# ReLU and row sum on one core: the first block cut from 16 to 15 rows a partition, so that all row pitches change

## The chip, the cores and the metric

The kernel runs on one core of one Trainium2 chip. The metric is the device time of one execution in microseconds (us), taken as the median over runs. Before the change it is 160.99 us, the median of three runs from 160.93 to 161.05.

## The reference

The input x has 32 x 512 x 1024 float32 numbers, 67.1 MB. The output has one float32 for each of the 16,384 rows of 1,024 numbers: the sum of the row after negative numbers were set to zero.

```
relu_x = np.maximum(x, 0)
return np.sum(relu_x, axis=-1)
```

Each number is read once and used twice (a maximum, an addition), so the work is a stream from the chip's memory (HBM) through the on-chip memory (SBUF) with very little written back.

## The kernel before, in words

The 16,384 rows are spread over 128 partitions, 128 rows (4 KB each) to a partition. The tensor is not cut evenly into 128 runs of 128 rows. It is cut in two regions (`xf` and `xv` in `relu_sum`). The first region holds 2,048 rows, and partition p gets 16 of them that follow each other in memory. So the rows of neighbouring partitions begin 64 KB apart: this distance is called the pitch. The second region holds the other 112 rows of each partition, again consecutive, at a pitch of 448 KB.

The work goes in blocks. Each of the seven blocks (`NB`) is one DMA load of 16 rows a partition, 64 KB to each partition and 8.4 MB in all, into one of three buffers `io0` to `io2`, which are used in turn. Block 0 is the first region; blocks 1 to 6 are the first 96 rows of the second region. The last 16 rows a partition are the **tail**, which is cut ever finer so that little is left to do after the last byte: a load of 8 rows, one of 4 rows, and four loads that share the last four rows: 2,302 numbers a partition (two rows and a piece of 254), 873 numbers (the far end of the four rows), 518 numbers, and 403 numbers, the last into a small buffer `last`.

All loads are issued by SyncE (SP) from one queue, in the order of the code (`load`, the DMA at L104). The first is moved ahead of the start of the program (`open_without_barrier`). Loads 0 to 2 wait for nothing; from the fourth on, a load waits until VectorE (DVE) is done with the block that was in the buffer (`freed`, a count of the semaphore `dve`). The first load of the tail waits so for block 4; those behind it wait only because SP issues in order.

The lists `TWO`, `ACT` and `DVE` say who computes each block. `TWO` lists groups of rows that pass through two engines: ScalarE (ACT) clamps the group in place (`clamp`, L145) and DVE adds it up (`total`, L153). `ACT` and `DVE` count rows that one engine does alone, clamp and sum in one instruction (`act_row`, L160; `dve_row`, L168). Blocks 0 and 1 are one group of 16, blocks 2 to 4 two groups of 8, block 5 two groups of 7 and two rows for ACT alone, block 6 eight rows for each engine alone. In the tail rows alternate between ACT and DVE; in the load of 8 rows the eighth goes to ACT too, so ACT has five and DVE three.

The last rows are computed in pieces: `act_part` (L122) and `dve_part` (L127) take the loads of 873 and 518 numbers, GpSimd (POOL) clamps a piece of 254 (L246), and one last DVE instruction (L266) and one last ACT instruction take the load of 403. Then SP stores the last two columns of `res` (`store`, L116). Two larger stores go before it. Eight matrix products (`multiply`, L186), whose result nobody reads, run on TensorE (PE) after the last block of the loop.

Of the kernel before, what the change touches and what calls it, by code (L numbers as in the profile page):

```python
# [4 lines left out]
F32 = mybir.dt.float32  # L5
RELU = mybir.ActivationFunctionType.Relu
MAX, ADD = mybir.AluOpType.max, mybir.AluOpType.add
P = 128

ROWS = 16  # L10
NBUF = 3


TWO = [[16], [16], [8, 8], [8, 8], [8, 8], [7, 7], []]
ACT = [0, 0, 0, 0, 0, 2, 8]
DVE = [0, 0, 0, 0, 0, 0, 8]

TAIL = [8, 4]  # L20

HEAD, MIDDLE = 254, 518
LAST_DVE, LAST_ACT = 252, 151
MIDDLE_ACT, END_ACT = 214, 321
# [29 lines left out]
class Semaphores:  # L56
    def __init__(self, tc: tile.TileContext):
        n = len(TWO) + len(TAIL) + 4
        self.loads = [tc.alloc_semaphore(f"load{i}") for i in range(n)]
        self.act = tc.alloc_semaphore("act")  # L60
        self.dve = tc.alloc_semaphore("dve")
        self.end = self.loads[-1]
        self.stored = tc.alloc_semaphore("stored")


def relu_sum(nc, sems: Semaphores, x: bass.AP, out: bass.AP):
    x_flat = x.flatten_outer_dims()
    N, D = x_flat.shape
    NT = N // P
    NB = len(TWO)  # L70
    assert N == P * NT == P * ROWS * (NB + 1)
    assert sum(TAIL) == ROWS - 4
    assert HEAD + MIDDLE + LAST_DVE == D and HEAD == 2 + LAST_DVE

    bufs = [nc.alloc_sbuf_tensor(f"io{i}", [P, ROWS, D], F32) for i in range(NBUF)]
    res = nc.alloc_sbuf_tensor("res", [P, NT], F32)


    n_last = LAST_DVE + LAST_ACT
    last = nc.alloc_sbuf_tensor("last", [P, 2 + n_last + 2], F32)  # L80


    N1 = P * ROWS
    xf = x_flat[:N1].rearrange("(p m) d -> p m d", p=P)
    xv = x_flat[N1:].rearrange("(p m) d -> p m d", p=P)
    o_flat = out.rearrange("b s -> (b s)")
    of = o_flat[:N1].rearrange("(p m) -> p m", p=P)
    ov = o_flat[N1:].rearrange("(p m) -> p m", p=P)

    def rows(m, n):  # L90
        if m < ROWS:
            return xf[:, m : m + n, :]
        return xv[:, m - ROWS : m - ROWS + n, :]

    def sums(m, n):
        if m < ROWS:
            return of[:, m : m + n], res[:, m : m + n]
        return ov[:, m - ROWS : m - ROWS + n], res[:, m : m + n]

    n_load = n_act = n_dve = n_store = 0  # L100

    def load(dst, src, after=None):
        nonlocal n_load
        dma = nc.sync.dma_start(out=dst, in_=src)  # L104
        if after:
            dma.wait_op(sems.dve, after[1], "sem-ge")
        dma.then_inc(sems.loads[n_load], 16)
        n_load += 1
        return sems.loads[n_load - 1]

    def store(m, n, act, sem, count):
        nonlocal n_store
        dst, src = sums(m, n)
        if act:
            nc.sync.wait_ge(sems.act, act)
        nc.sync.dma_start(out=dst, in_=src).wait_op(sem, count, "sem-ge").then_inc(  # L116
            sems.stored, 16
        )
        n_store += 1

    def act_part(ap, accum_out, after):
        nc.scalar.activation(out=ap, in_=ap, func=RELU, accum_out=accum_out).wait_op(  # L122
            *after, "sem-ge"
        ).then_inc(sems.end, 1)

    def dve_part(ap, accum_out, after):
        i = nc.vector.tensor_scalar(  # L127
            out=ap,
            in0=ap,
            scalar1=0.0,  # L130
            scalar2=None,
            op0=MAX,
            op1=ADD,
            accum_out=accum_out,
        )
        if after is not None:
            i.wait_op(*after, "sem-ge")
        i.then_inc(sems.end, 1)

    def clamp(ap, loaded):  # L140
        nonlocal n_act
        if n_act == 0:
            nc.scalar.preload_act_table(RELU).wait_op(loaded, 16, "sem-ge")  # L143
            loaded = None
        i = nc.scalar.activation(out=ap, in_=ap, func=RELU)  # L145
        if loaded is not None:
            i.wait_op(loaded, 16, "sem-ge")
        i.then_inc(sems.act, 1)
        n_act += 1

    def total(ap, m, n):
        nonlocal n_dve
        nc.vector.tensor_reduce(  # L153
            out=res[:, m : m + n], in_=ap, axis=mybir.AxisListType.X, op=ADD
        ).wait_op(sems.act, n_act, "sem-ge").then_inc(sems.dve, 1)
        n_dve += 1

    def act_row(ap, accum_out, loaded):
        nonlocal n_act
        i = nc.scalar.activation(out=ap, in_=ap, func=RELU, accum_out=accum_out)  # L160
        if loaded is not None:
            i.wait_op(loaded, 16, "sem-ge")
        i.then_inc(sems.act, 1)
        n_act += 1

    def dve_row(ap, accum_out, loaded):
        nonlocal n_dve
        i = nc.vector.tensor_scalar(  # L168
            out=ap,
            in0=ap,  # L170
            scalar1=0.0,
            scalar2=None,
            op0=MAX,
            op1=ADD,
            accum_out=accum_out,
        )
        if loaded is not None:
            i.wait_op(loaded, 16, "sem-ge")
        i.then_inc(sems.dve, 1)
        n_dve += 1  # L180

    def multiply(done):
        ps = nc.alloc_psum_tensor("ps", [P, MM_COLS], F32)
        rows_of = bufs[(NB - 2) % NBUF]
        for k in range(N_MM):
            i = nc.tensor.matmul(  # L186
                ps[:, :], rows_of[:, 0, :P], rows_of[:, 1, :MM_COLS], start=True, stop=True
            )
            if k == 0:
                i.wait_op(sems.dve, done, "sem-ge").then_inc(sems.end, 1)  # L190

    freed = []
    m = 0
    for j in range(NB):
        buf = bufs[j % NBUF]
        loaded = load(buf[:, :, :], rows(m, ROWS), j >= NBUF and freed[j - NBUF])
        c = 0
        act_waits = dve_waits = loaded
        for n in TWO[j]:
            clamp(buf[:, c : c + n, :], act_waits)  # L200
            total(buf[:, c : c + n, :], m + c, n)
            act_waits = None
            c += n
        for _ in range(ACT[j]):
            act_row(buf[:, c, :], res[:, m + c : m + c + 1], act_waits)
            act_waits = None
            c += 1
        for _ in range(DVE[j]):
            dve_row(buf[:, c, :], res[:, m + c : m + c + 1], dve_waits)
            dve_waits = None  # L210
            c += 1
        assert c == ROWS
        freed.append((n_act, n_dve))
        m += ROWS


    multiply(freed[-1][1])
    buf = bufs[NB % NBUF]
    c = 0
    for n in TAIL:  # L220
        loaded = load(
            buf[:, c : c + n, :], rows(m, n), None if c else freed[NB - NBUF]
        )
        for i in range(n):
            if i % 2 == 0 or (n == 8 and i == 7):
                act_row(buf[:, c, :], res[:, m : m + 1], loaded if i == 0 else None)
            else:
                dve_row(buf[:, c, :], res[:, m : m + 1], loaded if i == 1 else None)
            c += 1
            m += 1  # L230

    flat = buf[:, :, :].rearrange("p c d -> p (c d)")
    src = rows(m, 4).rearrange("p c d -> p (c d)")
    at = c * D
    head = 2 * D + HEAD
    middle = head + MIDDLE
    end = middle + n_last


    loaded = load(flat[:, at : at + head], src[:, :head])  # L240
    act_row(buf[:, c, :], res[:, m : m + 1], loaded)
    sums_act = n_act
    dve_row(buf[:, c + 1, :], res[:, m + 1 : m + 2], loaded)
    sums_dve = n_dve
# [1 line left out]
    nc.gpsimd.tensor_scalar(  # L246
        out=clamped, in0=clamped, scalar1=0.0, scalar2=None, op0=MAX
    ).wait_op(loaded, 16, "sem-ge").then_inc(sems.end, 1)
    for lo, hi, n, first, second in (
        (end, 4 * D, END_ACT, 2 + n_last, 3 + n_last),  # L250
        (head, middle, MIDDLE_ACT, 0, 1),
    ):
        loaded = load(flat[:, at + lo : at + hi], src[:, lo:hi])
        act_part(flat[:, at + lo : at + lo + n], last[:, first : first + 1], (loaded, 16))
        dve_part(flat[:, at + lo + n : at + hi], last[:, second : second + 1], (loaded, 16))
    loaded = load(last[:, 2 : 2 + n_last], src[:, middle:end])
    assert loaded is sems.end

    store(0, ROWS, freed[0][0], sems.dve, freed[0][1])
    store(ROWS, NT - ROWS - 2, sums_act, sems.dve, sums_dve)


    all_there = (sems.end, 16 + 6)
# [61 lines left out]
```

## Time and profile before

| what | before |
|---|---|
| time, median of three runs | 160.99 us (160.93 to 161.05) |
| span of the profiled execution, first to last instruction | 159.9 us |
| what lies around the span, if that execution took the median | 1.1 us |
| moved from HBM | 67.11 MB, 420 GB/s over the span |
| DMA packets' time as a share of 16 DMA engines | 97.8% |
| DVE busy | 118.7 us (74%) |
| ACT busy | 103.6 us (65%) |
| PE, POOL busy | 8.6 us, 1.0 us |

The time of the profiled execution itself is not recorded beside its span; sums are made against the span and carried over to the median with the 1.1 us unchanged. A packet here is one partition's share of one load, moved by one of the 16 DMA engines; a block of 16 rows is 128 packets of 64 KB, eight to each DMA engine. The chain of waits follows the work back from the last instruction, each step to what released it. The DMA view can be asked for a window of time: it divides the window into 40 slices, and its row "GB/s" puts the bytes of a packet into the slice in which the packet begins, so that in a short window the row shows when packets begin.

### The profile page before, as it was taken

How to read it: one execution, taken by the hardware profiler on the slowest of the kernel's cores; microseconds unless marked ns; L12 is line 12 of the kernel's file. 1: busy time of each engine (PE TensorE's matmuls, PEld its weight loads, DVE VectorE, ACT ScalarE, POOL GpSimd, SP SyncE). 2: the span in 40 equal slices, each digit the busy share in tenths (PEclk: the TensorE clock that was granted, in tenths of full speed). 3: DMA queues.
4: the chain of work that ended last, by engine and by line, in shares of the span. 5: the costliest groups of instructions: out<-in, count | busy, mean ns of one | idle time of the engine just before them, and what ended most of it. 6: DMA issues, size and time to landing. Idle time of an engine off the chain costs nothing.

```text
span 159.9 us, 157 instructions
## 1 busy us (share of the span) xinstructions
PE 8.6 (5%) x16; PEld 3.6 (2%) x16; DVE 118.7 (74%) x44; ACT 103.6 (65%) x53; POOL 1.0 (1%) x5
## 2 busy tenths in 40 slices
PE   0000000000000000000000000000000000000695
PEld 0000000000000000000000000000000000000241
DVE  0000000006999799999999999999999799999986
ACT  0000049993599807997099950999429993397995
POOL 0000000000000000000000000000000000000001
DMA  8996996996996997999979979969969969899993
GB/s 279 508 492 295 524 492 295 524 492 295 525 492 295 524 475 311 524 393 393 525 328 459 508 344 459 508 295 508 492 295 524 492 295 524 377 402 402 428 396 110
DMA packets 2304, 67.18 MB, mean 420 GB/s; under 512 B 640, under 2 KB 768, under 8 KB 1024
## 3 DMA queue, kind: packets, MB, share of 16 engines
q1 hardware_dynamic: 2304, 67.18, 97.8%
HBM read 67.11 MB, written 0.07 MB: 420 GB/s over the span
## 4 chain that ended last, share of the span: by engine, by line
DMA 45%; DVE 45%; ACT 9%; SPq 1%; issue 0%
DMA io<-in_x_dram 45%; DVE res L153 43%; ACT io L145 9%; DVE io L168 1%; SPq L104 1%; DVE io L127 1%; DVE io L266 0%
## 5 line engine op out<-in xcount | busy, mean ns | idle before, releaser
L153 DVE TENSOR_REDUCE res<-io 128x8 f32<-128x8192 f32 (+2 forms) x10 | 101.1, 10173 | 39.2 <-ACT io L145 39.2
L145 ACT ACTIVATE io<-io 128x8192 f32<-128x8192 f32 (+2 forms) x10 | 81.8, 8218 | 25.9 <-DMA io<-in_x_dram 25.9
L160 ACT ACTIVATE io<-io 128x1024 f32<-128x1024 f32 x18 | 18.8, 1042 | 6.6 <-DMA io<-in_x_dram 6.6
L186 PE MATMUL ps<-io 128*128 128x512 f32 x16 | 8.6, 698 | 149.5 <-DVE io L168 149.5
L168 DVE TENSOR_SCALAR_CACHE_REDUCE io<-io 128x1024 f32<-128x1024 f32 x14 | 16.2, 1215 | 0.5 <-DMA io<-in_x_dram 0.4
L143 ACT ACT_TABLE_LOAD x1 | 1.3, 1283 | 22.3 <-DMA io<-in_x_dram 22.3
L186 PEld LDWEIGHTS ps<-io 128*128 128x128 f32 x16 | 3.6, 231 | 153.7 <-DVE io L168 149.5
L160 ACT ACTIVATION_READ_ACCUMULATOR io<-io 128x1 f32 x18 | 3.3, 186 | 0.0
L246 POOL TENSOR_SCALAR io<-io 128x254 f32<-128x254 f32 x1 | 0.8, 841 | 155.4 <-DMA io<-in_x_dram 155.4
L168 DVE DVE_READ_ACCUMULATOR io<-io 128x1 f32 x14 | 1.2, 82 | 0.0
L127 DVE TENSOR_SCALAR_CACHE_REDUCE io<-io 128x552 f32<-128x552 f32 (+1 forms) x2 | 1.1, 594 | 0.0
L122 ACT ACTIVATE io<-io 128x321 f32<-128x321 f32 (+1 forms) x2 | 0.9, 426 | 0.1
L266 DVE SCALAR_TENSOR_TENSOR io<-last,io 128x254 f32<-128x254 f32 x1 | 0.4, 423 | 0.0
L122 ACT ACTIVATION_READ_ACCUMULATOR io<-io 128x1 f32 x2 | 0.4, 186 | 0.0
L122 ACT ACTIVATE last<-last 128x153 f32<-128x153 f32 x1 | 0.3, 330 | 0.0
L122 ACT ACTIVATION_READ_ACCUMULATOR last<-last 128x1 f32 x1 | 0.2, 187 | 0.0
L127 DVE DVE_READ_ACCUMULATOR io<-io 128x1 f32 x2 | 0.2, 82 | 0.0
L311 POOL MEMSET const-uint8-127<- 128x1 uint8 x1 | 0.1, 102 | 0.0
L311 POOL MEMSET const-bfloat16-1.0<- 128x1 bf16 x1 | 0.1, 101 | 0.0
L311 POOL MEMSET const-float32-0.0<- 128x1 f32 x1 | 0.1, 99 | 0.2 <-issue 0.2
L311 POOL MEMSET const-float32-1.0<- 128x1 f32 x1 | 0.1, 98 | 0.0
L266 DVE DVE_READ_ACCUMULATOR io<-last,io 128x1 f32 x1 | 0.1, 82 | 0.0
## 6 DMA issues: line engine op xcount, KB each, us to landing
io<-in_x_dram SPq DMA_DIRECT2D x1, 4096.0 KB, 23.7
io<-in_x_dram SPq DMA_DIRECT2D x1, 2048.0 KB, 28.3
io<-in_x_dram SPq DMA_DIRECT2D x1, 1151.0 KB, 30.6
io<-in_x_dram SPq DMA_DIRECT2D x1, 436.5 KB, 31.2
io<-in_x_dram SPq DMA_DIRECT2D x1, 259.0 KB, 31.4
last<-in_x_dram SPq DMA_DIRECT2D x1, 201.5 KB, 31.4
io<-in_x_dram SPq DMA_DIRECT2D x7, 29.0
out_dram<-res SPq DMA_DIRECT2D x1, 55.0 KB, 1.6
```

What stands on the lines that cost most here:

```text
L104: dma = nc.sync.dma_start(out=dst, in_=src)
L122: nc.scalar.activation(out=ap, in_=ap, func=RELU, accum_out=accum_out).wait_op(*after, "sem-ge").then_inc(sems.end, 1)
L127: i = nc.vector.tensor_scalar(out=ap, in0=ap, scalar1=0.0, scalar2=None, op0=MAX, op1=ADD, accum_out=accum_out,)
L143: nc.scalar.preload_act_table(RELU).wait_op(loaded, 16, "sem-ge")
L145: i = nc.scalar.activation(out=ap, in_=ap, func=RELU)
L153: nc.vector.tensor_reduce(out=res[:, m : m + n], in_=ap, axis=mybir.AxisListType.X, op=ADD).wait_op(sems.act, n_act, "sem-ge").then_inc(se ...
L160: i = nc.scalar.activation(out=ap, in_=ap, func=RELU, accum_out=accum_out)
L168: i = nc.vector.tensor_scalar(out=ap, in0=ap, scalar1=0.0, scalar2=None, op0=MAX, op1=ADD, accum_out=accum_out,)
L186: i = nc.tensor.matmul(ps[:, :], rows_of[:, 0, :P], rows_of[:, 1, :MM_COLS], start=True, stop=True)
L246: nc.gpsimd.tensor_scalar(out=clamped, in0=clamped, scalar1=0.0, scalar2=None, op0=MAX).wait_op(loaded, 16, "sem-ge").then_inc(sems.end, 1)
L266: nc.vector.scalar_tensor_tensor(out=clamped, in0=last[:, : 2 + LAST_DVE], scalar=0.0, in1=clamped, op0=MAX, op1=ADD, accum_out=res[:, NT ...
L311: nc = _bacc.Bacc("TRN2", target_bir_lowering=False, num_devices=1)
```

## The change

The first region gets 15 rows a partition in place of 16, so its pitch is 60 KB. The second region gets 113 rows at a pitch of 452 KB. Block 0 is 15 rows; blocks 1 to 6 stay at 16 rows; the tail grows from 16 rows to 17, and its first load from 8 rows to 9. Of these 9 rows ACT computes five and DVE four. As 17 rows do not fit in a buffer of 16, the load of 873 numbers goes to a buffer of its own, `ends`, and the two instructions on it work there. The stores are cut at 15 rows in place of 16. The rest of the last four rows is as before. Issue order, waits and semaphores stay.

```diff
+FIRST = 15
-TWO = [[16], [16], [8, 8], [8, 8], [8, 8], [7, 7], []]
+TWO = [[15], [16], [8, 8], [8, 8], [8, 8], [7, 7], []]
-TAIL = [8, 4]
+TAIL = [9, 4]
...
+    n_end = 2 * D - HEAD - MIDDLE - n_last
+    ends = nc.alloc_sbuf_tensor("ends", [P, n_end], F32)
-    N1 = P * ROWS
+    N1 = P * FIRST
     xf = x_flat[:N1].rearrange("(p m) d -> p m d", p=P)
     xv = x_flat[N1:].rearrange("(p m) d -> p m d", p=P)
...
-        loaded = load(buf[:, :, :], rows(m, ROWS), j >= NBUF and freed[j - NBUF])
+        n_rows = sum(TWO[j]) + ACT[j] + DVE[j]
+        loaded = load(buf[:, :n_rows, :], rows(m, n_rows), j >= NBUF and freed[j - NBUF])
...
-            if i % 2 == 0 or (n == 8 and i == 7):
+            if i % 2 == 0:
...
-    for lo, hi, n, first, second in (
-        (end, 4 * D, END_ACT, 2 + n_last, 3 + n_last),
-        (head, middle, MIDDLE_ACT, 0, 1),
+    for dst, lo, hi, n, first, second in (
+        (ends[:, :], end, 4 * D, END_ACT, 2 + n_last, 3 + n_last),
+        (flat[:, at + head : at + middle], head, middle, MIDDLE_ACT, 0, 1),
     ):
-        loaded = load(flat[:, at + lo : at + hi], src[:, lo:hi])
+        loaded = load(dst, src[:, lo:hi])
...
-    store(0, ROWS, freed[0][0], sems.dve, freed[0][1])
-    store(ROWS, NT - ROWS - 2, sums_act, sems.dve, sums_dve)
+    store(0, FIRST, freed[0][0], sems.dve, freed[0][1])
+    store(FIRST, NT - FIRST - 2, sums_act, sems.dve, sums_dve)
```

More of the change, by code (lines that the diff above doesn't have):

```diff
@@ L70, in relu_sum @@
     NB = len(TWO)
-    assert N == P * NT == P * ROWS * (NB + 1)
-    assert sum(TAIL) == ROWS - 4
+    assert N == P * NT
+    assert FIRST + ROWS * (NB - 1) + sum(TAIL) + 4 == NT
+    assert sum(TAIL) * D + 2 * D + HEAD + MIDDLE <= ROWS * D
     assert HEAD + MIDDLE + LAST_DVE == D and HEAD == 2 + LAST_DVE
@@ L90, in rows @@
     def rows(m, n):
-        if m < ROWS:
+        if m < FIRST:
             return xf[:, m : m + n, :]
-        return xv[:, m - ROWS : m - ROWS + n, :]
+        return xv[:, m - FIRST : m - FIRST + n, :]
     def sums(m, n):
-        if m < ROWS:
+        if m < FIRST:
             return of[:, m : m + n], res[:, m : m + n]
-        return ov[:, m - ROWS : m - ROWS + n], res[:, m : m + n]
+        return ov[:, m - FIRST : m - FIRST + n], res[:, m : m + n]
     n_load = n_act = n_dve = n_store = 0
@@ L211, in relu_sum @@
             c += 1
-        assert c == ROWS
+        assert c == n_rows
         freed.append((n_act, n_dve))
-        m += ROWS
+        m += n_rows
     multiply(freed[-1][1])
@@ L248, in relu_sum @@
     ).wait_op(loaded, 16, "sem-ge").then_inc(sems.end, 1)
-    for lo, hi, n, first, second in (
-        (end, 4 * D, END_ACT, 2 + n_last, 3 + n_last),
-        (head, middle, MIDDLE_ACT, 0, 1),
-    ):
-        loaded = load(flat[:, at + lo : at + hi], src[:, lo:hi])
-        act_part(flat[:, at + lo : at + lo + n], last[:, first : first + 1], (loaded, 16))
-        dve_part(flat[:, at + lo + n : at + hi], last[:, second : second + 1], (loaded, 16))
+    assert end + n_end == 4 * D
+    for dst, lo, hi, n, first, second in (
+        (ends[:, :], end, 4 * D, END_ACT, 2 + n_last, 3 + n_last),
+        (flat[:, at + head : at + middle], head, middle, MIDDLE_ACT, 0, 1),
+    ):
+        loaded = load(dst, src[:, lo:hi])
+        act_part(dst[:, :n], last[:, first : first + 1], (loaded, 16))
+        dve_part(dst[:, n:], last[:, second : second + 1], (loaded, 16))
     loaded = load(last[:, 2 : 2 + n_last], src[:, middle:end])
     assert loaded is sems.end
-    store(0, ROWS, freed[0][0], sems.dve, freed[0][1])
-    store(ROWS, NT - ROWS - 2, sums_act, sems.dve, sums_dve)
+    store(0, FIRST, freed[0][0], sems.dve, freed[0][1])
+    store(FIRST, NT - FIRST - 2, sums_act, sems.dve, sums_dve)
     all_there = (sems.end, 16 + 6)
```

## The prediction

> **What bounds the kernel now.** I read the chain of waits first, then the timeline of DVE at the end, then the DMA view in short windows, at the start and far behind it.
>
> The chain (start us, length us, what) runs through DVE in its middle:
>
> ```profile
> 0.43 41.14 DMA io<-in_x_dram
> ...
> 55.49 68.79 DVE res L153 x7
> ...
> 124.29 0.33 SPq L104
> ...
> 125.15 30.57 DMA io<-in_x_dram
> ```
>
> It looks as if DVE's sums (L153) set the end, because their last releases the tail's load at 124.29. But that load only has to be in the queue before block 6 is there. ACT's first row of block 6 starts at 138.35 (timeline, ended by a DMA), so the load has 14 us to spare. The other refills, by the timeline of SP and ACT's starts: 54.70 against 60.95 (block 2 landed), 72.73 against 80.29, 89.92 against 99.65, 107.11 against 118.99. The smallest margin is 6.2 us. So the DMA queue never runs dry, and the transfers are the bound. Blocks land at 41.6, 60.95, 80.29, 99.65, 118.99, 138.35: one every 19.35 us.
>
> The end of DVE's timeline shows the stream still ahead of the engines:
>
> ```profile
> 154.10 1.22 DVE L168 TENSOR_SCALAR_CACHE_REDUCE io<-io 128x1024 f32<-128x1024 f32 x1
> 155.24 0.08 DVE L168 DVE_READ_ACCUMULATOR io<-io 128x1 f32 x1
> 155.75 1.22 DVE L168 TENSOR_SCALAR_CACHE_REDUCE io<-io 128x1024 f32<-128x1024 f32 x1 [0.42 <-DMA io<-in_x_dram]
> ...
> 157.93 0.08 DVE L127 DVE_READ_ACCUMULATOR io<-io 128x1 f32 x1
> 158.05 0.42 DVE L266 SCALAR_TENSOR_TENSOR io<-last,io 128x254 f32<-128x254 f32 x1
> ```
>
> DVE waits 0.42 us for a load at 155.75, and its last instruction starts at 158.05, when the last load has landed; 0.5 us of DVE and 1.4 us of store follow. The reader is to see that DVE is free at 158.01, only 0.04 us before.
>
> Now the DMA itself. First window, 0 to 3.97 us, in which each engine begins its first packet; second window, 3.97 to 6.39 us, its second packet; then, at 134.57 to 136.99 us, the last packet of block 6:
>
> ```profile
> DMA packets 16, 1.05 MB, mean 264 GB/s; under 512 B 0, under 2 KB 0, under 8 KB 0
> ...
> q1 hardware_dynamic: 16, 1.05, 77.3%
> ```
>
> ```profile
> GB/s 1083 2166 1083 0 1083 4333 3250 1083 1083 0 0 0 0 0 1083 0 1083 0 0 0 0 0 0 0 0 0 0 0 0 0 0 0 0 0 0 0 0 0 0 0
> ...
> q1 hardware_dynamic: 16, 1.05, 99.9%
> ```
>
> ```profile
> GB/s 2166 2166 0 1083 4333 4333 0 1083 0 0 0 0 0 1083 0 1083 0 0 0 0 0 0 0 0 0 0 0 0 0 0 0 0 0 0 0 0 0 0 0 0
> ...
> q1 hardware_dynamic: 16, 1.05, 100.0%
> ```
>
> The share times the window is the mean packet, as each engine has one: 77.3% of 3.97 is 3.07 us for the first, 99.9% of 2.42 is 2.42 us for the second, and 2.42 us for the one 130 us later. Only the first packet is slow, by 0.65 us in the mean. One packet is 1083 GB/s in a slice of 0.0605 us: in the second window 14 engines begin within nine slices, up to 4.51 us, one in slice 15 and the last in slice 17, at 4.94 to 5.00 us. In the third window the two laggards are still there, at the same distance. So the order and the lag that the engines have after their first packet stay to the end, and the slowest engine's end of its first packet plus a fixed amount of work is the time of the kernel.
>
> **The change part by part.** Bytes first. Each engine moves the same bytes in the same number of packets (nothing is added to the 2304 of the page), eight 60 KB packets for eight of 64 KB in block 0 and eight of 36 KB for eight of 32 KB in the tail: 8 x (2.42 x 15/16) is 1.21 us less, and the ninth row gives it back. **0.0 us at the end.**
>
> Block 0 lands 1.21 us earlier, and so does every load up to block 6; the tail's first load lands when it did, near 148.0. That is what the engines feel:
> - ACT's clamp of block 0: 13.86 us for 16 rows, 13.95 for two of 8 rows, so about 13.0 for 15. DVE's sum of block 0: 17.22 less 1.07 (half of a group of 16 less one of 8, 17.22 - 8.68 = 8.54 for 8 rows) is 16.15 us. Both start 1.2 us sooner; covered, as refills have 6 us or more.
> - From block 1 on DVE's sums follow each other (55.49 to 124.28) and move 1.2 us forward with the landing of block 1. The refills keep or widen their margins; block 0's is released near 51.5 for a landing near 59.7.
> - In the tail DVE has one row more: 1.14 us from start to start (149.37 to 150.51). It begins block 6's rows 1.2 us earlier (near 139.05 for 140.26), so after twelve rows it is done near 152.8, as before (152.87). The following load of 4 rows lands near 152.9 still. That cover is thin, 0.1 us; if it went, DVE would be late by the missing part, at most the 1.14 us of a row, and 0.42 us of the wait at 155.3 would take it up first. ACT has five rows as before.
> - The 873 numbers in `ends`, the stores of 15 and 111 columns, the other clamps: same instructions on same sizes, 0.0 us. The earlier start of the idle matrix products (149.51, near 148.3 after) is waited for by nobody late: they need 8.6 us, but only the first one counts in the last semaphore.
> No wait is added, and nothing moves in SP's or POOL's queue.
>
> So two terms are left, and both are of the pitch. **Pitch of the first block, in the first packet.** No row shows 60 KB. Above: the DMA records of the trace, taken packet by packet, have starts from 1.01 to 1.84 us and lengths of 2.63 to 3.38 us; the slowest end is at 4.98 us. The latest start with the longest packet would be 1.84 + 3.38 = 5.22 us, +0.24 us. Below: the two laggards level with the others (8 slices) is -0.48 us; the latest start with no excess at all is 1.84 + 2.42 = 4.26, -0.72 us. Nearest row: packets 2 to 8 of the same load, at the same pitch, show no excess, so the pitch of 64 KB as such costs nothing; what is slow is the start. I take 0.0 us.
>
> **Pitch of the rest, in about 56 rounds of packets** (six blocks of eight, and 17 rows of tail). Below, nothing can come: the rounds of before are at one speed, 2.42 us for both pitches, the one of 64 KB and the one of 448 KB. Above, the slowest later round in the trace, at 124.84 to 127.26 us while SP issues the tail's loads:
>
> ```profile
> q1 hardware_dynamic: 16, 1.05, 102.0%
> ```
>
> 102.0% of 2.42 is 2.47 us, 0.05 more; in all 56 rounds that would be +2.8 us. Nearest are the rows at 448 KB, 1% away in pitch. I take 0.0 us.
>
> The Trainium skill, "DMA: Bandwidth & Descriptors", section "Latency and other measured facts", in its row on HBM row pitch, says that pitches of 2 MiB and more lose speed, that 512 KiB does not, and that 4 KiB added to a slow pitch brings it back. By that rule 448 KB has nothing to regain from the 4 KB that this change adds, and the sum stays at zero; the trace agrees with its 2.42 us in every round but the first.
>
> The sum is 0.0 us on a span of 159.9, hence 161.0 us as the median is now. About 0.2% (0.32 us) either way is what a measurement of this kernel can tell from no change.
>
> **The rivals.**
> A. The slow first packet is a collision: sixteen streams that begin nearly together at addresses a multiple of 64 KB apart get in each other's way until they are staggered, and then no longer. At 60 KB they start apart. For it: the excess is there only in the round in which the engines begin together, and is unequal, 0.2 to 1.0 us. Against: other costs of a beginning would look the same. Price: -0.48 us if the laggards fall in with the rest, **160.5 us**, at most -0.72, 160.3. DVE would let it through: it moves with the landings, and its 0.42 us of wait is left for what does not. The same page of the Trainium skill names, as an unproved inference, that streams in lock-step meet on the same memory channel; the trace neither shows nor excludes it.
> B. Slower: at 452 KB, engines in their stagger of about 1 us meet each other in memory where at 448 KB they do not. Place: the rounds of blocks 1 to 6 and the tail. Price: up to 2.8 us, **163.8 us**, by the disturbed round; a third of that, 161.9 us, is as likely. It decides from 0.32 / 56 = 6 ns a packet, from 2.418 to 2.424 us. Against: all 48 rounds at 448 KB run at the speed of block 0 at a quite different pitch.
> C. The change does what it says, but the start falls otherwise by chance (+0.24 us at most): inside the band of no change.
>
> **How the numbers follow.** Forecast with C, within 0.2%: 0.40, 160.7 to 161.3. A: 0.34. B: 0.26, about half of it above 162.0, since small losses and the whole row are equally open. The range takes in A down to its full price and B's lower half: 160.3 to 162.0, leaving out about 0.15.
>
> **What would show it.** Right: a second window with the two laggards in their slices, 2.42 us in later rounds, blocks from the second on landing 1.2 us sooner up to block 6, the 9-row load near 148.0. A would show as a mean first packet well under 3.07 - 0.15 us (60 KB takes 2.27 at full speed) and laggards within nine slices; B as a share over 100.2% in windows of later rounds and blocks more than 19.35 us apart. Wrong in another way would be a DVE wait gone at 155.75, with DVE and not the load ahead of the last instruction.

## The result and the profile after

The changed kernel takes 161.40 us, the median of nine runs, against 160.99 us; the ratio is 1.0023 with a 95% interval from 1.0014 to 1.0032. That is 0.4 us slower, just beyond the 0.2% that the prediction called no change, and inside its range. One of the nine, at 192.67 us, stood apart from the others (161.20 to 161.46 us) and does not enter the ratio.

The chain of waits of the changed kernel (start us, length us, what) has the same links as before:

```profile
0.43 39.91 DMA io<-in_x_dram
...
54.25 68.79 DVE res L157 x7
...
123.06 0.33 SPq L108
...
123.92 31.78 DMA io<-in_x_dram
```

Block 1 is there at 40.34 us for 41.57, DVE's row of sums starts 1.24 us sooner, and so does the issue of the tail. At the end, in the timeline of DVE, nothing is left of that:

```profile
151.57 1.21 DVE L172 TENSOR_SCALAR_CACHE_REDUCE io<-io 128x1024 f32<-128x1024 f32 x1
152.71 0.08 DVE L172 DVE_READ_ACCUMULATOR io<-io 128x1 f32 x1
152.93 1.22 DVE L172 TENSOR_SCALAR_CACHE_REDUCE io<-io 128x1024 f32<-128x1024 f32 x1
...
155.72 1.22 DVE L172 TENSOR_SCALAR_CACHE_REDUCE io<-io 128x1024 f32<-128x1024 f32 x1 [0.43 <-DMA io<-in_x_dram]
...
158.03 0.42 DVE L272 SCALAR_TENSOR_TENSOR io<-last,io 128x254 f32<-128x254 f32 x1
```

The reader is to see that DVE, with a row more to do, still waits: 0.14 us before 152.93 and 0.43 us before 155.72. DVE's last instruction starts at 158.03 as the last load lands, 0.02 us from where it did.

So the two profiles have the same span, 159.94 and 159.93 us, while the medians differ by 0.4 us. Either the difference lies outside the span, or one of the two profiles is not typical. The first runs decide that.

Two terms carry the rest of this text. The **lag** is the time between the first and the last of the 16 DMA engines to finish block 0, by the landings in the trace. The second is what lies around the span: the time of a profiled run less its span.

### The profile page after: what moved, and what is told of

Same layout as the page of the kernel before. It is cut to its first block, busy times and chain, and to the rows that moved or that the text cites. A ratio compares the mean times of both kernels' runs of the same rounds, so it can differ in the third digit from the quotient of the medians.

```text
span 159.9 us, 159 instructions
## 1 busy us (share of the span) xinstructions
PE 10.2 (6%) x16; PEld 4.1 (3%) x16; DVE 118.8 (74%) x46; ACT 102.7 (64%) x53; POOL 1.0 (1%) x5
## 4 chain that ended last, share of the span: by engine, by line
DMA 45%; DVE 45%; ACT 9%; SPq 1%; issue 0%
DMA io<-in_x_dram 45%; DVE res L157 43%; ACT io L149 9%; DVE io L172 1%; SPq L108 1%; DVE ends L131 0%; DVE io L272 0%; DVE io L131 0%
## 5 line engine op out<-in xcount | busy, mean ns | idle before, releaser
L157 DVE TENSOR_REDUCE res<-io 128x8 f32<-128x8192 f32 (+3 forms) x10 | 100.1, 10066 | 39.0 <-ACT io L149 39.0
L149 ACT ACTIVATE io<-io 128x8192 f32<-128x8192 f32 (+3 forms) x10 | 80.9, 8132 | 26.7 <-DMA io<-in_x_dram 26.7
L190 PE MATMUL ps<-io 128*128 128x512 f32 x16 | 10.2, 804 | 148.3 <-DVE io L172 148.3
L172 DVE TENSOR_SCALAR_CACHE_REDUCE io<-io 128x1024 f32<-128x1024 f32 x15 | 17.3, 1214 | 0.6 <-DMA io<-in_x_dram 0.4
L131 DVE TENSOR_SCALAR_CACHE_REDUCE ends<-ends 128x552 f32<-128x552 f32 x1 | 0.7, 725 | 0.0
L126 ACT ACTIVATE ends<-ends 128x321 f32<-128x321 f32 x1 | 0.5, 472 | 0.0
L131 DVE TENSOR_SCALAR_CACHE_REDUCE io<-io 128x304 f32<-128x304 f32 x1 | 0.5, 470 | 0.0
```

The lines of the kernel that those rows point to most:

```text
L131: i = nc.vector.tensor_scalar(out=ap, in0=ap, scalar1=0.0, scalar2=None, op0=MAX, op1=ADD, accum_out=accum_out,)
L157: nc.vector.tensor_reduce(out=res[:, m : m + n], in_=ap, axis=mybir.AxisListType.X, op=ADD).wait_op(sems.act, n_act, "sem-ge").then_inc(se ...
L172: i = nc.vector.tensor_scalar(out=ap, in0=ap, scalar1=0.0, scalar2=None, op0=MAX, op1=ADD, accum_out=accum_out,)
L190: i = nc.tensor.matmul(ps[:, :], rows_of[:, 0, :P], rows_of[:, 1, :MM_COLS], start=True, stop=True)
```

## Experiments

All were timed in five rounds beside the kernel before, in three groups (e1 to e4, e5 to e8, e9 to e12), each on one chip of its own. The kernel before had medians of 161.00, 160.99 and 160.98 us in them. "Time" is the median of a kernel's runs; the ratio is the one on record against the kernel before, and is not simply the quotient of the two medians. The last three columns, in us, are of one profiled run, so a lag is that of a single execution.

| kernel | pitch of block 0, KB | of the rest, KB | time, us | ratio and 95% interval | its own time | span | lag |
|---|---|---|---|---|---|---|---|
| e1 before again | 64 | 448 | 160.91 | 0.9994 (0.9986 to 1.0003) | 160.87 | 159.54 | 0.52 |
| e2 sizes alone | 64 | 448 | 161.13 | 1.0005 (0.9996 to 1.0014) | 161.03 | 159.71 | 0.55 |
| e3 pitches alone | 60 | 452 | 161.37 | 1.0019 (1.0011 to 1.0028) | 161.40 | 160.08 | 1.01 |
| e4 after again | 60 | 452 | 161.43 | 1.0026 (1.0016 to 1.0035) | 161.42 | 160.06 | 0.89 |
| e5 first pitch | 60 | 448 | 161.49 | 1.0027 (1.0018 to 1.0036) | 161.23 | 159.87 | 0.81 |
| e6 rest's pitch | 64 | 452 | 161.00 | 0.9997 (0.9989 to 1.0006) | 161.12 | 159.80 | 0.60 |
| e7 first pitch | 68 | 448 | 161.40 | 1.0024 (1.0014 to 1.0035) | 161.29 | 159.96 | 0.73 |
| e8 first pitch | 128 | 448 | 160.95 | 0.9997 (0.9988 to 1.0006) | 160.90 | 159.57 | 0.39 |
| e9 shifted 4 KB | 64 | 448 | 160.92 | 1.0003 (0.9994 to 1.0012) | 161.00 | 159.64 | 0.55 |
| e10 shifted 32 KB | 64 | 448 | 160.78 | 0.9994 (0.9985 to 1.0002) | 160.77 | 159.45 | 0.51 |
| e11 first pitch | 96 | 448 | 161.29 | 1.0019 (1.0010 to 1.0029) | 161.43 | 160.09 | 1.05 |
| e12 one region | 512 | 512 | 161.49 | 1.0037 (1.0025 to 1.0050) | 161.49 | 160.13 | 1.05 |

The profile shown of before has a lag of 0.99 us, that of after 0.90 us with a span of 159.93 and a time of 161.25 us.

### Addresses or sizes, inside the span or outside (e1 to e4)

e1 is the kernel before and e4 the changed one, without an edit. e2 is the changed program with the old addresses:

```diff
-            return xf[:, m : m + n, :]
-        return xv[:, m - FIRST : m - FIRST + n, :]
+            return bass.AP(x_flat.tensor, m * D, [[16 * D, P], [D, n], [1, D]])
+        row = 2048 + m - FIRST - (m >= NT - 17)
+        return bass.AP(x_flat.tensor, row * D, [[112 * D, P], [D, n], [1, D]])
```

e3 is the old program with the new addresses:

```diff
-            return xf[:, m : m + n, :]
-        return xv[:, m - ROWS : m - ROWS + n, :]
+            return bass.AP(x_flat.tensor, m * D, [[15 * D, P], [D, n], [1, D]])
+        row = 1920 + m - ROWS
+        return bass.AP(x_flat.tensor, row * D, [[113 * D, P], [D, n], [1, D]])
```

Expected of e1:

> The kernel before once more, as a measure of the noise and to learn its own times beside its spans. Every theory expects 161.0 us and a ratio of 1.000. What is to be read is what lies around the span. Theory AROUND (the profiled spans of before and after are alike, 159.94 and 159.93 us, so the 0.4 us of the change lies before the first or after the last instruction) expects a time 1.0 to 1.1 us above the span here and 1.3 us after the change. Theory STREAM (the streaming part itself is longer in most executions, and the profiled one was a good one) expects 1.3 us here too, so spans of 159.6 to 159.8.

Of e2:

> The sizes of the change (15 rows first, 17 in the tail, the buffer for 873 numbers) at the pitches of before, 64 and 448 KB. The sixteenth row of each partition's first region is not read, and one row of the second region is read twice. Theory PITCH (addresses make the 0.4 us): 161.0 us, as before. Theory SIZES (the program and its instructions make it): 161.4 us, as after.

Of e3:

> The program of before with its sizes, reading at the pitches of the change, 60 and 452 KB. One row of each partition is read twice and the last one is not read. Theory PITCH: 161.4 us. Theory SIZES: 161.0 us. By STREAM a first round of packets that ends later than 4.98 us, by AROUND a span of 159.9 whatever the time.

Of e4:

> The changed kernel once more on the same chip as the three others. Every theory expects 161.4 us, ratio 1.0023. AROUND expects spans of 159.9 to 160.1 with the time 1.3 us above them, and the kernel before with the same spans and 1.05 us above them; STREAM expects spans 0.3 to 0.4 us longer than those of the kernel before.

Measured: what lies around the span is 1.33 us in e1, 1.32 in e2 and e3, 1.36 in e4 (own time less span, in the table). AROUND falls. The profile of before, with its span of 159.94, was then an execution of about 161.27 us (159.94 + 1.33, worked out), beyond the 161.05 of the slowest of its nine timed runs. Of the 90 timed runs of the kernel before in the three groups, eight took 161.25 us or more. e1 shows a usual one: span 159.54. Of the pair that divides the change, e3 carries it (1.0019) and e2 does not show one (1.0005, interval across 1). PITCH stands, and SIZES falls as the cause of the whole; the interval of e2 still leaves room for up to 0.2 us (0.0014 of 161) of it.

Where the time sits is seen in the DMA view of one window, 3.9 to 5.2 us, cut in slices of 0.0325 us. As explained above, a number stands where a packet begins, here each engine's second. First e1, then e3:

```profile
GB/s 0 0 0 0 2016 0 2016 2016 0 2016 4033 6049 2016 2016 2016 4033 0 0 2016 0 2016 0 0 0 0 0 0 0 0 0 0 0 0 0 0 0 0 0 0 0
```

```profile
GB/s 0 0 0 0 0 2016 0 0 4033 2016 0 0 0 4033 0 2016 0 0 4033 0 0 2016 2016 2016 2016 2016 0 0 0 0 0 2016 0 0 0 2016 0 0 0 0
```

2016 GB/s is one packet. In e1 the 16 engines begin within slices 5 to 21, 0.52 us from first to last (16 steps of 0.0325); in e3 within slices 6 to 36, 0.98 us. The first engine is at the same place; the last is 15 slices later, 0.49 us. The spans differ by 0.54 us (160.08 - 159.54). The profile of before in the same window is of the second kind, which is why it hid the change:

```profile
GB/s 0 0 2016 0 2016 2016 2016 0 0 0 0 6049 4033 4033 2016 2016 0 0 2016 0 0 0 0 0 0 0 0 0 0 2016 0 0 0 2016 0 0 0 0 0 0
```

### First packets or all packets (e5, e6), and which pitches (e7, e8)

All four are the program of before with another factor in one of its two addresses: 15 rows for block 0 (e5), 113 rows for the rest, from row 1920 (e6), 17 and 32 rows for block 0 (e7, e8). As in e5:

```diff
-            return xf[:, m : m + n, :]
-        return xv[:, m - ROWS : m - ROWS + n, :]
+            return bass.AP(x_flat.tensor, m * D, [[15 * D, P], [D, n], [1, D]])
+        row = 2048 + m - ROWS
+        return bass.AP(x_flat.tensor, row * D, [[112 * D, P], [D, n], [1, D]])
```

Expected of e5:

> The program and sizes of before; only the first block is read at a pitch of 60 KB, the rest at 448 KB as before. The sixteenth row of a partition's first block is also the first of the next partition's, so some rows are read twice and some not. Theory FIRST (the 0.4 us are made in the first packets, while sixteen engines start together): 161.4 us, the slowest engine 0.9 to 1.0 us behind the first when block 0 lands and still so at the last load. Theory REST (the pitch of 452 KB slows later packets): 161.0 us and 0.5 us.

Of e6:

> The program and sizes of before; the first block at 64 KB as before, only the rest at 452 KB, starting 128 rows earlier, so that some rows are read twice and some not. Theory FIRST: 161.0 us, lag of 0.5 us at block 0 and at the last load. Theory REST: 161.4 us, with packets of more than 2.42 us or a lag that grows after block 0.

Of e7:

> As before, only the first block at a pitch of 68 KB (17 rows), so some rows are read twice and some not. Theory EVEN (pitches that are multiples of 64 KB start best): 161.4 us and a lag of 0.9 to 1.0 us. Theory DENSE (the closer the first addresses, the worse): 161.0 us or a little less.

Of e8:

> As before, only the first block at a pitch of 128 KB (32 rows), so some rows are read twice and some not. Theory EVEN: 161.0 us, a lag of 0.5 us. Theory DENSE: 160.8 us or less, lag under 0.4 us. Should an unlucky few addresses decide and no rule of the pitch, e7 and e8 fall anywhere between 160.8 and 161.5.

Measured: e5 takes 161.49 us and e6 161.00 us. Block 0's pitch alone brings the whole loss (1.0027), the rest's pitch none (0.9997). FIRST stands, REST falls. ACT's first instruction waits for block 0 and shows when it landed (timeline; first e1, then e5):

```profile
21.84 1.28 ACT L143 ACT_TABLE_LOAD   x1 [21.84 <-DMA io<-in_x_dram]
```

```profile
22.18 1.28 ACT L144 ACT_TABLE_LOAD   x1 [22.18 <-DMA io<-in_x_dram]
```

Block 0 is there 0.34 us later in e5, and the span is 0.33 us longer (159.87 - 159.54). The last packets of block 6, at 452 KB, run at full speed in the changed kernel; DMA view of after, 133.45 to 135.87 us:

```profile
DMA packets 16, 1.05 MB, mean 433 GB/s; under 512 B 0, under 2 KB 0, under 8 KB 0
## 3 DMA queue, kind: packets, MB, share of 16 engines
q1 hardware_dynamic: 16, 1.05, 99.9%
```

Packet by packet, the DMA records of block 1 on give a mean of 2.421 us for a 64 KB packet both before and after, and 2.424 us in e6. The lag in e5 is 0.81 us, below the 0.9 to 1.0 expected, in an execution (161.23 us) that is the fastest of its eleven.

68 KB is slow (1.0024), 128 KB is not (0.9997). EVEN forecast both times; DENSE falls with e7. The window 3.9 to 5.2 us of e8:

```profile
GB/s 0 0 0 0 0 0 0 0 0 2016 4033 6049 0 2016 4033 2016 4033 0 2016 2016 0 4033 0 0 0 0 0 0 0 0 0 0 0 0 0 0 0 0 0 0
```

All engines begin within slices 10 to 22, and no straggler follows. Yet the first engine is 0.16 us later than in e1, and so the kernel is not faster.

### Edges or steps (e9 to e12)

e9 and e10 move block 0 by one and by eight rows at 64 KB; e11 has 24 rows as its pitch; e12 has one region of 128 rows a partition for everything.

```diff
-            return xf[:, m : m + n, :]
+            return bass.AP(x_flat.tensor, (m + 1) * D, [[16 * D, P], [D, n], [1, D]])
```

```diff
-    xf = x_flat[:N1].rearrange("(p m) d -> p m d", p=P)
-    xv = x_flat[N1:].rearrange("(p m) d -> p m d", p=P)
+    xa = x_flat.rearrange("(p m) d -> p m d", p=P)
...
-        if m < ROWS:
-            return xf[:, m : m + n, :]
-        return xv[:, m - ROWS : m - ROWS + n, :]
+        return xa[:, m : m + n, :]
```

Expected of e9:

> As before at 64 and 448 KB, only the first block begins 4 KB (one row) further on, so every one of its packets begins 4 KB past a multiple of 64 KB, counted from the beginning of x; one row of the first region is not read and one is read twice. Theory EDGE (a first packet is slow to start where its 64 KB do not begin at a multiple of 64 KB): 161.4 us, a lag of 0.7 to 1.0 us between the first and the last engine at block 0. Theory STEP (the distance between the engines' addresses decides, whatever they begin at): 161.0 us and 0.4 to 0.5 us.

Of e10:

> The same with a shift of 32 KB (eight rows). EDGE with an edge every 64 KB: 161.4 us. EDGE with one every 32 KB or less, or STEP: 161.0 us.

Of e11:

> As before, only the first block at a pitch of 96 KB (24 rows), no shift; some rows are read twice and some not. Every second partition begins at an odd multiple of 32 KB. STEP with multiples of 64 KB only: 161.4 us. EDGE every 64 KB: about 161.4 us or something between, as the partitions that begin the load are even and odd ones; EDGE every 32 KB: 161.0 us.

Of e12:

> One region only, 128 rows a partition at a pitch of 512 KB for every block; sizes and program as before. Both EDGE and STEP expect 161.0 us and a lag near 0.5 us, since 512 KB is a multiple of 64 KB. If the two regions of before are worth something by themselves, it is slower.

Measured: both shifts at 64 KB are as fast as before (1.0003 and 0.9994), so EDGE falls: a packet that begins off a multiple of 64 KB of x is not slower for it. 96 KB is slow (1.0019), as STEP has it. But 512 KB is slow too (1.0037), against STEP, with a lag of 1.05 us that is already there at block 0. The window 3.9 to 5.2 us of e12:

```profile
GB/s 0 2016 0 0 0 0 2016 4033 0 0 0 0 2016 0 2016 0 2016 2016 0 2016 0 0 2016 0 2016 0 0 2016 0 4033 0 0 0 0 2016 0 2016 0 0 0
```

From slice 2 to slice 37 is 1.14 us: one engine is early, and the others are spread over 0.98 us (slices 7 to 37) instead of the half microsecond of e1. So of six pitches for block 0, 64 and 128 KB are the good ones, 60, 68, 96 and 512 KB the bad ones. STEP as I put it (any multiple of 64 KB) falls with the last; e12 also moved the rest to 512 KB, and was not tried with the first block alone.

None of the twelve beats both kernels by more than its interval; the lowest, e10 (160.78 us, 0.9985 to 1.0002), isn't shown to differ from before.

## Why the prediction was right, and where it was not

**The stream is the bound, and each engine's lag after its first packet stays to the end: right.** In the 14 profiles at hand the span less the lag at block 0 lies between 158.9 and 159.2 us, while the lag goes from 0.39 to 1.05 us. The landing of block 0 on its slowest engine tells still more, because the first engine, from which the lag counts, is not always done at the same time. From there to the end of the span it is 137.7 to 137.8 us in all eleven profiles with 16 rows in block 0, and 138.9 to 139.0 in the three with 15 (landings in the trace). The difference is the 1.2 us that the prediction has for the row moved to the tail. What a pitch costs is thus in place, to about 0.1 us, when block 0 has landed.

**The sizes cost nothing: not contradicted.** e2 has them at the old addresses, 1.0005 (0.9996 to 1.0014), so up to 0.2 us is not excluded. The steps were near the mark: DVE's sum of 15 rows was put at 16.15 us and takes 16.15; block 0's refill was put at 51.5 and is issued at 51.55; block 2 lands at 59.72 for 59.7; the load of nine rows is there at 148.04, put at 148.0. The thin cover of DVE in the tail, 0.1 us, is 0.14 us.

**The pitch of the rest, taken as 0.0: right.** Rival B falls with e6 (0.9997), and a 64 KB packet takes 2.421 us at 448 KB before and at 452 KB after. The 2.424 us of e6 are not the pitch: e6 has single packets of up to 2.60 us, while in e3 and e4, at the same 452 KB, the longest is 2.49 and the mean 2.420 to 2.421 (DMA records). The prediction's "every round but the first" leaves out its own round of 2.47 us while SP issues the tail's loads. Such a round is there in all 14 profiles (2.45 to 2.47 us, DMA records in windows of 2.42 us), so it makes no difference between the kernels. The Trainium skill, "DMA: Bandwidth & Descriptors", section "Latency and other measured facts", says in its row on HBM row pitch that 4 KiB added to a pitch of 4 MiB brought back the full rate. Here 448 KB had no loss to win back, and 4 KB more won nothing. The row gives rates of whole copies and is silent on the first packet of a load.

**Inside the range by luck.** The forecast proper ended at 161.3 us. That the range reached up to the measured 161.40 was for rival B's sake, and B is refuted.

**The pitch of the first block in the first packet, taken as 0.0: here the sum failed.** e5 has this term alone: 161.49 against 160.99 us, +0.5 us by the medians, +0.43 us by the ratio (0.0027 of 160.99). The argument was that packets 2 to 8 of block 0 show no excess at 64 KB, so the pitch as such costs nothing. That says only that a pitch is harmless once the engines are staggered. It says nothing about what another pitch does while they start, and this was the one place where the trace showed a loss. The upper bound, +0.24 us, failed too, by where it was counted from. Its end of the slowest first packet, 5.22 us, is passed in no profile (5.07 us in e3, 5.13 in e11, DMA records), though single packets are longer than the 3.38 us it took: 3.97 us in e3, 3.81 in e4. But the 4.98 us from which it counted belong to an execution of about 161.27 us. In e1 the slowest engine ends its first packet at 4.58 us, and from there the same 5.22 is +0.64 us.

**Rival A had the place and the wrong sign.** The price hangs on the first packets, as A said, and a pitch changes the time by 0.3 to 0.6 us (ratios of e5, e7, e11 and e12); but 64 KB is among the good pitches, and 60 KB among the bad ones. A's cause, sixteen streams that collide when they begin a multiple of 64 KB apart, is refuted as it stood: 60 and 68 KB (e5, e7) are slower, and 128 KB (e8) has the smallest lag, 0.39 us.

**The reference profile.** The time around the span was put at 1.1 us by setting a span against a median of other executions. It is 1.32 to 1.36 us in the 13 profiles with a time of their own. That the changed kernel's profile came out at the span that was forecast, 159.93 for 159.9 us, is luck: an execution of the kernel before that lay above its median met one of the changed kernel (161.25 us) that lay below its own. The two laggards in the fences of the prediction, 0.48 us behind, were a feature of that execution; in e1 the last engine is two slices, 0.07 us, behind the next. Of the 0.48 us that rival A promised, 0.28 (161.27 less 160.99) were thus already in the median.

**What stays open** is why a pitch is good or bad. The mean length of the first packet hardly tells: 3.10 us in e8 and 3.11 us in e12 (DMA records), one at a good and one at a bad pitch. What differs is how many engines are late. Of the profiles with 64 KB first packets, at most two of 16 engines end theirs after 4.60 us at 64 and 128 KB, and four to seven at 60, 68, 96 and 512 KB. Collisions in memory at the start are a possible cause, and no run here shows them. The records also do not say which partition an engine takes first, so how far apart the engines' first addresses lie is not known, nor where x lies in memory.

## What to carry to other kernels

When a stream runs at one speed from its second packet on, as here, look at the first: there the engines got their order and their lag, and the last of them set the end. A parameter that leaves the steady rate alone can still move the start, so its cost there has to be bounded by more than the rows of one execution. And a single profile may be an unusual execution: its span means little against another one until its own time stands beside its own median.

## What the runs showed of the hardware

- The address step between partitions in the first load alone moved the whole kernel by 0.3 to 0.4 us of 161 (ratios 1.0019 to 1.0027 in e5, e7, e11), through the slowest of 16 DMA engines; 452 for 448 KB in the later loads alone moved nothing that was measured (0.9997 in e6).
- The lag is not made up: in e11 it is 1.05 us at block 0 and, by the landings in the trace, 1.00 us at the last load, 136 us later.
- Single later packets of up to 2.60 us for 2.42 occurred in e6 and up to 2.63 us in e12 (DMA records). They cost about 0.1 us at most: from the landing of block 0 to the end it is 137.84 us in e6 and 137.79 in e12, for 137.69 to 137.76 in the other nine profiles with 16 rows in block 0.
